# Stick-breaking attention: the causal mask moves from a matrix product into the scan

## The chip, the cores and the metric

The kernel runs on one core of a Trainium2 chip. The metric is the device time of one execution in microseconds, and the median of several runs is given. The engines are TensorE (PE; its weight loads are PEld), VectorE (DVE), ScalarE (ACT), GpSimd (POOL) and SyncE (SP, which here only starts transfers). Each works through its own instructions in a fixed order.

## The reference

Two decoder layers over 512 tokens of width 1024, all in float32. Each layer is a half-step FFN, a mixer, and another half-step FFN, each behind an RMSNorm. Layer 0 mixes with gated linear attention, layer 1 with stick-breaking attention, 16 heads of width 64. Only the second mixer is touched by the change:

```python
z = jnp.einsum('bhtd,bhsd->bhts', q_blk, k).astype(jnp.float32) * scale
mask = s_pos[None, :] < t_pos[:, None]
sp = jnp.where(mask, jax.nn.softplus(z), 0.0)
rem = lax.cumsum(sp, axis=3, reverse=True) - sp
weights = jnp.where(mask, jnp.exp(jax.nn.log_sigmoid(z) - rem), 0.0)
return jnp.einsum('bhts,bhsd->bhtd', weights.astype(v.dtype), v)
```

As `log_sigmoid(z)` is `z - softplus(z)`, a visible weight is `exp(z - S)`, where `S` is the sum of softplus from this key to the last visible one. The mask is strict: a query sees only keys in front of it.

## The kernel before, in words

Every large product is made of three products in a rounded format (a high part times a high part, and the two mixed ones), so each weight tile is split before use: ACT rounds the raw tile to `wh` (line 152) and DVE subtracts to get `wl` (line 153). The products themselves are line 80 (and lines 412 and 779 in the FFNs). Such a split is needed for each 128x1024 piece of weights.

The mixer (class `SB`) runs 17 steps. Step `s` makes the logarithms of the weights of head `s` (`weights_log`) and turns those of head `s-1` into weights (`weights`). After every second head, `values` multiplies two heads by their value vectors. Between these pieces PE is fed with the input and output projections of the mixer by `feed.halves`, so that PE has work while ACT and DVE are busy on a head. `evac_q` and `evac_k` bring the projections of a pair of heads out of PSUM (`n`), and `parts` splits them into `mq`, `kh` and `kl` on ACT and DVE.

The 512 queries of a head are four tiles of 128, and tile `i` needs keys of `i+1` blocks of 128. They are packed into three PSUM tiles `ps_z` of 384, 384 and 512 columns: tile 2; tiles 1 and 0; tile 3. For each of the three, in this order:

- PE makes the logits `z` (line 1486), and adds -1e30 to the masked keys with one more product of an identity `idb` and a triangle `negm` in bfloat16 (`mask`). From step 5 on, the mask of the first two tiles is written first, one step ahead (`masks`).
- ACT makes `|z|` (line 1529), `exp(-|z|)` and `ln(1 + ...)` (through `act`, line 656) into `l`, and `max(z, 0)` into `r` (Relu, line 1532). Their sum is softplus.
- DVE sums from the last key to the first with a scan for each query tile (line 1535), which takes `r` and `l` and adds both at each key, and subtracts the result from the logits (line 1543), which frees the PSUM tile.

One step later PE transposes the result (line 1557), ACT takes the exponential into `wt` (line 656), and `values` uses it (line 1572). ACT then rounds its result to `oh` (line 1581) and DVE makes `ol` (line 1582).

PSUM has three buffers for `ps_z`. The order of the instructions on each engine is fixed when the program is built, by a scheduler that takes code order, priorities and estimated durations; `tc.issue_after` puts an instruction no earlier than another.

Of the kernel before, what the change touches and what calls it, by code (L numbers as in the profile page):

```python
# [10 lines left out]
F32 = mybir.dt.float32  # L11
F32R = mybir.dt.float32r
BF16 = mybir.dt.bfloat16
U8 = mybir.dt.uint8
AF = mybir.ActivationFunctionType
ALU = mybir.AluOpType
PSUM = bass.MemoryType.PSUM

P = 128
T = 512  # L20
# [6 lines left out]
NEG = -1.0e30  # L27
# [3 lines left out]
def turns(t):  # L31

    return t.rearrange("p (two n) -> p n two", two=2)
# [13 lines left out]
def decoder(ctx: ExitStack, tc: tile.TileContext, a: dict, out: bass.AP):  # L47
    nc = tc.nc
# [12 lines left out]
    def psum(name, tag=None):  # L61
        if tag is None:
            tag = order[turn_[0] % 8]
            turn_[0] += 1
        return pp.tile([P, T], F32, tag=tag, bufs=banks[tag], name=name)


    ident = cp.tile([P, P], F32, name="ident")
# [458 lines left out]
    st = {}  # L527
# [125 lines left out]
    def act(o, i, fn, **kw):  # L653

        with tc.issue_after(st["tab"]):
            st["last"] = nc.scalar.activation(o, i, fn, **kw).ins


    class FFN:
# [328 lines left out]
        def run(self, between=None):  # L988
            with tc.tile_pool(name="hp", bufs=8, reuse_waits="tile") as self.hp, tc.tile_pool(
                name="tp", bufs=5, reuse_waits="tile"  # L990
            ) as self.tp:
                st["few"] = self.hp
                new_norm()
                if st["ss"] is not None:
                    if self.after_ffn:
                        exp_ln_tables(st["closed"])
                    two_halves(lambda after: sums_wide(self.tp, after))
                    rstd_wide()
                flush(self.defer)
                def spread(todo, n):  # L1000
                    for i in range(n):
                        for piece in todo[i * len(todo) // n : (i + 1) * len(todo) // n]:
                            with behind(self.last_up):
                                piece()
                        feed.entries(1)

                spread(self.normed_input(), self.NORMED - 2)
                self.normed = True
                st["h"], st["l"] = zip(*self.n)
                st["made"] = [k for j in range(4) for k in (j, j + 4)]  # L1010
                todo = self.sums()
                spread(todo[:5], self.sums_by - self.NORMED)
                feed.entries(1, True)
                for piece in todo[5:]:
                    piece()
                feed.entries(self.count - self.sums_by - 1, True)
                if between is not None:
                    with tc.issue_after(st["closed"]):
                        nc.scalar.preload_act_table_set("sqrt_and_others")
                    feed.q[feed.pos].split()  # L1020
                    between(self.tp)
                feed.entries(self.total - self.count)
# [380 lines left out]
    class SB:  # L1403
# [81 lines left out]
        def logits(self, o_, l_, r_, first, last=False):  # L1485
            nc.tensor.matmul(o_, l_, r_, start=first, stop=last, skip_group_check=True)  # L1486

        def mask(self, bk, ps, first):

            w = self.WID[bk]  # L1490
            m0 = P if bk == 2 else w - P
            nb = (w - m0) // P
            self.logits(
                ps[:, m0:w].rearrange("p (n s) -> p n s", n=nb),
                self.idb,
                self.negm.unsqueeze(1).to_broadcast([P, nb, P]),
                first,
                not first,
            )

        def masks(self, s):


            if self.AHEAD <= s < 16:
                for bk in (1, 2):
                    self.zs[bk] = psum("ps_z", "z")
                    self.mask(bk, self.zs[bk], True)

        def weights_log(self, p, e):

            m = self.qk[p, e, "q"]
            kh, kl = self.qk[p, e, "k"]
            self.ys[p, e] = ys = [None] * 3
            for bk, tiles in ((1, (2,)), (2, (1, 0)), (0, (3,))):
                ahead = bk in self.zs
                ps = self.zs.pop(bk) if ahead else psum("ps_z", "z")
                w = self.WID[bk]
                for n_, i in enumerate(tiles):

                    c0, n = self.BK[i][1], max(2, i + 1) * P  # L1520
                    ts_ = slice(i * P, (i + 1) * P)
                    o_, h_, l_ = ps[:, c0 : c0 + n], turns(kh)[:, 0 : n // 2], turns(kl)[:, 0 : n // 2]
                    self.logits(o_, m[:, ts_], h_, n_ == 0 and not ahead)
                    self.logits(o_, m[:, ts_], l_, False, ahead and i == tiles[-1])
                if not ahead:
                    self.mask(bk, ps, False)
                r = self.hp.tile([P, w], F32, tag=f"r{bk}", name="r")
                l = self.hp.tile([P, w], F32, tag=f"l{bk}", bufs=1, name="l")
                nc.scalar.activation(l, ps[:, 0:w], AF.Abs)
                act(l, l, AF.Exp, scale=-1.0)  # L1530
                act(l, l, AF.Ln, bias=1.0)
                st["relu"] = nc.scalar.activation(r, ps[:, 0:w], AF.Relu).ins
                for i in tiles:
                    c = slice(self.BK[i][1], self.BK[i][1] + (i + 1) * P)
                    nc.vector.tensor_tensor_scan(
                        out=l[:, c][:, ::-1],
                        data0=r[:, c][:, ::-1],
                        data1=l[:, c][:, ::-1],
                        initial=0.0,
                        op0=ALU.add,  # L1540
                        op1=ALU.add,
                    )
                nc.vector.tensor_tensor(out=r, in0=ps[:, 0:w], in1=l, op=ALU.subtract)
                ys[bk] = r
                yield
# [39 lines left out]
        def run(self):  # L1585
            with ExitStack() as es:
                vp = es.enter_context(tc.tile_pool(name="vp2", bufs=1, reuse_waits="tile"))
                self.op = es.enter_context(tc.tile_pool(name="op", bufs=8, reuse_waits="tile"))
                self.qp = es.enter_context(tc.tile_pool(name="qp2", bufs=4, reuse_waits="tile"))
                self.hp = es.enter_context(tc.tile_pool(name="hp3", bufs=2, reuse_waits="tile"))  # L1590
                self.v = [vp.tile([P, D], F32, name=f"w{i}") for i in range(NT)]
                self.ys, self.wt, self.zs = {}, {}, {}
                self.later, self.hold = [], False
                self.idb = vp.tile([P, P], BF16, name="idb")
                self.negm = vp.tile([P, P], BF16, name="negm")
                nc.vector.tensor_copy(self.idb, ident)
                nc.gpsimd.dma_start(self.negm, a["c_neg"])
                new_norm()
                two_halves()
                stats_a("t")  # L1600
                feed.step(2)
                stats_b("t")
                exp_ln_tables(st["sqrt"])
                flush(self.defer)
                feed.step(4)

                steps = [6] * 5 + [5] * 10 + [4] * 2
                self.hold = True
                for s in range(17):
                    p, e = divmod(s, 2)  # L1610
                    q, f = divmod(s - 1, 2)
                    n = steps[s]
                    if s < 16:
                        for i, _ in enumerate(self.weights_log(p, e)):
                            if i != 1:
                                self.parts(st["relu"])
                            if i == 1:
                                k = 2 if n > 4 else 1
                                feed.halves(k)
                                n -= k  # L1620
                    if s > 0:
                        for i, _ in enumerate(self.weights(q, f)):
                            if i < 2:
                                k = min(n, n % 2 if i == 0 and n % 2 else 2)
                                feed.halves(k)
                                n -= k
                            if i == 1:
                                self.masks(s + 1)
                        feed.halves(n)
                        if f == 1:  # L1630
                            self.values(q)
                    else:
                        feed.halves(n)
                feed.entries(self.end + 2 - feed.pos)
# [364 lines left out]
```

## Time and profile before

| | |
|---|---|
| median of 3 runs | 1762.55 us (1762.22 to 1762.95) |
| the profiled execution | 1762.8 us, its span 1760.9 us |
| granted TensorE clock | 0.999 |
| busy share of the span | PE 99%, PEld 93%, DVE 86%, ACT 60%, POOL 3% |
| the 17 steps of the mixer | about 1223 to 1400 us of the span |

A row of instructions names the line, the engine, the operation, what it writes and reads, the shape, how often it ran, the busy time and the mean of one. A row of the timeline begins with start and duration in us; in brackets at its end stand the idle time of the engine before it and what ended that. Records of neighbouring instructions can overlap by a little. In the order of a program, a scan is listed as SCALAR_TENSOR_TENSOR, as the other instructions with three inputs are.

### The profile page before, as it was taken

What the parts mean: (1) busy time and instruction counts of PE and PEld (TensorE: products, weight loads), DVE (VectorE), ACT (ScalarE), POOL (GpSimd) and SP (SyncE); (2) the same over time, 40 slices, a digit from 0 to 9 for tenths busy, and PEclk for the clock granted to TensorE, in tenths of its full rate; (3) what the DMA queues carried; (4) which work ended last, traced back from release to release, by engine and by line L of the source; (5) the groups of instructions that cost most, each with busy time, mean ns of one, the idle gap of its engine ahead of it and who ended that gap; (6) DMA issues with size and microseconds to landing.
All of it is one profiled execution on the core that took longest, in us unless ns stands there. A gap on an engine that the chain in (4) does not pass through costs nothing.

```text
span 1760.9 us, 31387 instructions
## 1 busy us (share of the span) xinstructions
PE 1749.1 (99%) x12714; PEld 1631.3 (93%) x12714; DVE 1509.2 (86%) x2490; ACT 1063.8 (60%) x1899; POOL 55.6 (3%) x77
## 2 busy tenths in 40 slices
PE   9999999999999999999999999999999999999998
PEld 8999999889888999999989999999888889999997
DVE  8999797786888999889798988977898679998886
ACT  7556556554665565555655555655888755565555
POOL 0000000200000000000000000010000000000000
PEclk9999999999999999999999999999999999999999
DMA  5533435422123443444434344352212234434351
GB/s 169 155 113 116 134 107 148 116 65 70 60 79 113 122 118 121 120 121 126 128 98 134 103 126 129 106 133 84 84 49 73 72 96 132 126 102 124 117 146 52
DMA packets 186389, 193.14 MB, mean 110 GB/s; under 512 B 4931, under 2 KB 171125, under 8 KB 186245
## 3 DMA queue, kind: packets, MB, share of 16 engines
q1 hardware_dynamic: 177760, 175.91, 32.0%
q0 software_dynamic: 8240, 14.95, 4.7%
q8 instruction: 99, 1.62, 0.4%
q14 instruction: 46, 0.37, 0.1%
q10 hardware_dynamic: 244, 0.29, 0.0%
HBM read 175.17 MB, written 2.10 MB: 101 GB/s over the span
## 4 chain that ended last, share of the span: by engine, by line
PE 89%; DVE 7%; ACT 3%; DMA 1%; issue 1%; DVEq 0%; SPq 0%
PE ps_w L779 21%; PE ps_d L80 15%; PE ps_f L80 14%; PE ps_q L779 10%; PE ps_z L779 5%; PE ps_w L412 5%; PE ps_b L80 4%; PE ps_t L80 4%; PE ps_q L412 2%; PE ps_z L412 1%; DVE wl L153 1%; PE ps_z L1486 1%; PE ps_oT L1572 1%; PE ps_bt L80 1%; PE ps_T L1557 1%; DMA raw<-in_ffn_w_gate_dram 1%
## 5 line engine op out<-in xcount | busy, mean ns | idle before, releaser
L153 DVE TENSOR_TENSOR wl<-raw,wh 128x1024 fp32r<-128x1024 f32 x241 | 256.4, 1065 | 37.0 <-ACT wh L152 36.2
L152 ACT CAST wh<-raw 128x1024 fp32r<-128x1024 f32 x241 | 222.2, 923 | 70.0 <-PE ps_f L80 23.6
L153 DVE TENSOR_TENSOR wl<-s,wh 128x1024 fp32r<-128x1024 f32 x160 | 195.8, 1224 | 66.2 <-ACT wh L152 65.3
L779 PE MATMUL ps_w<-th,wh 128*128 128x256 f32 x864 | 239.1, 277 | 0.2 <-ACT ps_z L807 0.2
L779 PE MATMUL ps_w<-tl,wh 128*128 128x256 f32 x864 | 237.8, 275 | 0.0
L779 PE MATMUL ps_w<-th,wl 128*128 128x256 f32 x864 | 237.8, 275 | 0.0
L152 ACT CAST wh<-s 128x1024 fp32r<-128x1024 f32 x160 | 168.8, 1055 | 6.0 <-DVE s L765 6.0
L779 PEld LDWEIGHTS ps_w<-th,wh 128*128 128x128 f32 x864 | 165.9, 192 | 1.1 <-ACT ps_z L807 0.4
L80 PE MATMUL ps_f<-xh,wh 128*128 128x512 f32 x432 | 166.5, 386 | 0.0
L779 PEld LDWEIGHTS ps_w<-tl,wh 128*128 128x128 f32 x864 | 166.0, 192 | 0.0
L779 PEld LDWEIGHTS ps_w<-th,wl 128*128 128x128 f32 x864 | 166.0, 192 | 0.0
L80 PE MATMUL ps_f<-xh,wl 128*128 128x512 f32 x432 | 164.3, 380 | 0.5 <-DVE wl L153 0.5
L80 PE MATMUL ps_f<-xl,wh 128*128 128x512 f32 x432 | 164.0, 380 | 0.0
L80 PE MATMUL ps_d<-hh,wh 128*128 128x512 f32 x416 | 157.9, 380 | 0.0
L80 PE MATMUL ps_d<-hh,wl 128*128 128x512 f32 x416 | 157.8, 379 | 0.0
L80 PE MATMUL ps_d<-hl,wh 128*128 128x512 f32 x416 | 157.8, 379 | 0.0
L153 DVE TENSOR_TENSOR wl<-rawd,wh 128x1024 fp32r<-128x1024 f32 (+1 forms) x100 | 96.6, 966 | 9.7 <-ACT wh L152 9.7
L807 ACT COPY ps_z<-ps_w 128x256 f32<-128x256 f32 x72 | 26.0, 362 | 118.3 <-PE ps_w L779 118.1
L363 POOL DMA_DIRECT2D x<-d x53 | 46.0, 911 | 1552.1 <-ACT d L362 1093.5
L80 PEld LDWEIGHTS ps_f<-xl,wh 128*128 128x128 f32 x432 | 81.8, 189 | 11.4
L80 PEld LDWEIGHTS ps_f<-xh,wl 128*128 128x128 f32 x432 | 81.8, 189 | 11.3 <-DVE wl L153 0.9
L80 PEld LDWEIGHTS ps_f<-xh,wh 128*128 128x128 f32 x432 | 81.8, 189 | 10.7
(357 smaller groups left out, 5437.9 us busy)
## 6 DMA issues: line engine op xcount, KB each, us to landing
raw<-in_ffn_w_gate_dram SPq DMA_DIRECT2D x43, 1024.0 KB, 5.5
raw<-in_ffn_w_up_dram SPq DMA_DIRECT2D x43, 1024.0 KB, 5.4
rawd<-in_ffn_w_down_dram SPq DMA_DIRECT2D x84, 512.0 KB, 4.0
x<-d POOLq DMA_DIRECT2D x53, 256.0 KB, 4.6
raw<-in_gla_w_in_dram SPq DMA_DIRECT2D x12, 1024.0 KB, 5.3
raw<-in_sb_w_in_dram SPq DMA_DIRECT2D x16, 512.0 KB, 3.7
raw<-in_gla_w_out_dram SPq DMA_DIRECT2D x4, 1024.0 KB, 5.4
raw<-in_sb_w_in_dram SPq DMA_DIRECT2D x4, 1024.0 KB, 5.1
```

The lines of the kernel that those rows point to most:

```text
L80: st["pe"] = nc.tensor.matmul(ps, l, r, start=first, stop=last).ins
L152: nc.scalar.copy(h[:, k], part)
L153: nc.vector.tensor_tensor(out=l[:, k], in0=part, in1=h[:, k].bitcast(F32), op=ALU.subtract)
L363: nc.gpsimd.dma_start(xs[k], d, accum_op=ALU.add)
L412: st["pe"] = nc.tensor.matmul(ps, l_, r_, start=first and c + n == 0, stop=c == 1 and n == 2, skip_group_check=True).ins
L779: st["pe"] = nc.tensor.matmul(o, l_, r_, start=first and j + n == 0, stop=j == 3 and n == 2, skip_group_check=True).ins
L807: v["copied"] = nc.scalar.copy(z, w).ins
L1486: nc.tensor.matmul(o_, l_, r_, start=first, stop=last, skip_group_check=True)
L1557: nc.tensor.transpose(ps[:, c0 : c0 + P], ys[yb][:, yc + j * P : yc + (j + 1) * P], ident)
L1572: nc.tensor.matmul(po[e * 64 : e * 64 + 64, j * P : T], self.v[j][:, c : c + 64], self.wt[p, e][bk][:, c0 : c0 + n], start=j == 0, stop=j ...
```

## The change

The mask is no longer added to the logits. The scan does the masking: instead of adding `r` and `l` at each key, it multiplies its running value by `keep` and adds `l`. The running value starts at 1e30, `keep` is 1 everywhere except for a 0 at the last visible key of each query. So from the end of the row to that key the running value stays at 1e30, at that key it becomes `l` alone, and from there on it sums. One tile `keep` serves all query tiles, which read different slices of it. As the scan has only two inputs and one of them is now `keep`, softplus must be complete before it: ACT's Relu goes, and a new DVE instruction computes `max(z, 0) + l` from PSUM. The two constants `idb` and `negm` give way to `keep`, made by a GpSimd memset and one DVE instruction ahead of the steps. The casts of `parts` now follow the logarithm (`st["logs"]`) instead of Relu.

```diff
-        def mask(self, bk, ps, first):
-
-            w = self.WID[bk]
-            m0 = P if bk == 2 else w - P
-            nb = (w - m0) // P
-            self.logits(
-                ps[:, m0:w].rearrange("p (n s) -> p n s", n=nb),
-                self.idb,
-                self.negm.unsqueeze(1).to_broadcast([P, nb, P]),
-                first,
-                not first,
-            )
-
-        def masks(self, s):
-
-
-            if self.AHEAD <= s < 16:
-                for bk in (1, 2):
-                    self.zs[bk] = psum("ps_z", "z")
-                    self.mask(bk, self.zs[bk], True)
-
         def weights_log(self, p, e):
...
-                ahead = bk in self.zs
-                ps = self.zs.pop(bk) if ahead else psum("ps_z", "z")
+                ps = psum("ps_z", "z")
...
-                    self.logits(o_, m[:, ts_], h_, n_ == 0 and not ahead)
-                    self.logits(o_, m[:, ts_], l_, False, ahead and i == tiles[-1])
-                if not ahead:
-                    self.mask(bk, ps, False)
+                    self.logits(o_, m[:, ts_], h_, n_ == 0)
+                    self.logits(o_, m[:, ts_], l_, False, i == tiles[-1])
...
                 nc.scalar.activation(l, ps[:, 0:w], AF.Abs)
                 act(l, l, AF.Exp, scale=-1.0)
                 act(l, l, AF.Ln, bias=1.0)
-                st["relu"] = nc.scalar.activation(r, ps[:, 0:w], AF.Relu).ins
+                st["logs"] = st["last"]
+                nc.vector.scalar_tensor_tensor(out=l, in0=ps[:, 0:w], scalar=0.0, in1=l, op0=ALU.max, op1=ALU.add)
                 for i in tiles:
                     c = slice(self.BK[i][1], self.BK[i][1] + (i + 1) * P)
                     nc.vector.tensor_tensor_scan(
                         out=l[:, c][:, ::-1],
-                        data0=r[:, c][:, ::-1],
+                        data0=self.keep[:, T - (i + 1) * P :][:, ::-1],
                         data1=l[:, c][:, ::-1],
-                        initial=0.0,
-                        op0=ALU.add,
+                        initial=-NEG,
+                        op0=ALU.mult,
                         op1=ALU.add,
                     )
...
-                self.idb = vp.tile([P, P], BF16, name="idb")
-                self.negm = vp.tile([P, P], BF16, name="negm")
-                nc.vector.tensor_copy(self.idb, ident)
-                nc.gpsimd.dma_start(self.negm, a["c_neg"])
+                self.keep = vp.tile([P, T], F32, name="keep")
+                nc.gpsimd.memset(self.keep, 1.0)
+                c = slice(T - P - 1, T - 1)
+                nc.vector.tensor_scalar(
+                    out=self.keep[:, c], in0=ident, scalar1=-1.0, scalar2=1.0, op0=ALU.mult, op1=ALU.add
+                )
...
-                                self.parts(st["relu"])
+                                self.parts(st["logs"])
...
-                            if i == 1:
-                                self.masks(s + 1)
```

In the order of the instructions, PE keeps every other instruction in its place. At the start of the steps, the difference on PE (`ps_z<-kh,mq` and `ps_z<-kl,mq` are the logits, `ps_z<-negm,idb` the mask with its own weight load):

```order
 L1486 MATMUL ps_z<-kh,mq 128x384
 L1486 MATMUL ps_z<-kl,mq 128x384
-L1486 LDWEIGHTS idb
-L1486 MATMUL ps_z<-negm,idb 128x128
 L1486 MATMUL ps_z<-kh,mq 128x256
 L1486 MATMUL ps_z<-kl,mq 128x256
 L1486 MATMUL ps_z<-kh,mq 128x256
 L1486 MATMUL ps_z<-kl,mq 128x256
-L1486 LDWEIGHTS idb
-L1486 MATMUL ps_z<-negm,idb 128x256
 L80 MATMUL ps_f<-xh,wh 128x512
```

The logits stand where they stood, and the two masks behind them are gone; the whole program has 48 such pairs fewer.

On DVE in step 1, before the change (`l<-r,l` are the scans, `r<-ps_z,l` the subtractions, `kl`, `n` and `mq` belong to the next pair of heads, `wl` to a weight tile):

```order
L1535 SCALAR_TENSOR_TENSOR l<-r,l 128x384
L1468 CAST kl<-kl 64x512
L1543 TENSOR_TENSOR r<-ps_z,l 128x384
L1467 TENSOR_TENSOR kl<-n,kh 64x512
L1434 SCALAR_TENSOR_TENSOR n<-ps_f,R 128x512
L1468 CAST kl<-kl 64x512
L1535 SCALAR_TENSOR_TENSOR l<-r,l 128x256
L1535 SCALAR_TENSOR_TENSOR l<-r,l 128x128
L153 TENSOR_TENSOR wl<-raw,wh 128x1024
L1543 TENSOR_TENSOR r<-ps_z,l 128x384
```

Each scan or pair of scans follows work of the next heads, and its subtraction comes soon after it. The same place in the changed program, where `l<-ps_z,l` is the new instruction and `l<-keep,l` the scan:

```order
L1509 SCALAR_TENSOR_TENSOR l<-ps_z,l 128x384
L1467 TENSOR_TENSOR kl<-n,kh 64x512
L1512 SCALAR_TENSOR_TENSOR l<-keep,l 128x384
L1468 CAST kl<-kl 64x512
L1520 TENSOR_TENSOR r<-ps_z,l 128x384
L1467 TENSOR_TENSOR kl<-n,kh 64x512
L1509 SCALAR_TENSOR_TENSOR l<-ps_z,l 128x384
L1468 CAST kl<-kl 64x512
L1512 SCALAR_TENSOR_TENSOR l<-keep,l 128x256
L1512 SCALAR_TENSOR_TENSOR l<-keep,l 128x128
L1434 SCALAR_TENSOR_TENSOR n<-ps_f,R 128x512
L1520 TENSOR_TENSOR r<-ps_z,l 128x384
```

Each PSUM tile has gained one instruction in front of its scans, often with another instruction between the two, and the `wl` of this place has moved further back. There are 48 new instructions in all.

More of the change, by code (lines that the diff above doesn't have):

```diff
@@ L1591, in run @@
                 self.v = [vp.tile([P, D], F32, name=f"w{i}") for i in range(NT)]
-                self.ys, self.wt, self.zs = {}, {}, {}
+                self.ys, self.wt = {}, {}
                 self.later, self.hold = [], False
-                self.idb = vp.tile([P, P], BF16, name="idb")
-                self.negm = vp.tile([P, P], BF16, name="negm")
-                nc.vector.tensor_copy(self.idb, ident)
-                nc.gpsimd.dma_start(self.negm, a["c_neg"])
+                self.keep = vp.tile([P, T], F32, name="keep")
[4 more added lines that the diff above has]
+                )
                 new_norm()
```

## The prediction

> **What bounds the kernel now.** I read the page first: shares of the engines, slices, chain.
>
> ```profile
> PE 1749.1 (99%) x12714; PEld 1631.3 (93%) x12714; DVE 1509.2 (86%) x2490; ACT 1063.8 (60%) x1899; POOL 55.6 (3%) x77
> DVE  8999797786888999889798988977898679998886
> PE 89%; DVE 7%; ACT 3%; DMA 1%; issue 1%; DVEq 0%; SPq 0%
> ```
>
> PE is never without work, and the chain that ended last is 89% PE. Read from this alone, whatever PE sheds is gained. But the change works in one stage of a tenth of the span, slices 29 to 32, and there DVE stands at 8, 9, 8 and 6 tenths. So the second view is the table by stretches, over the steps from the first logits (1223.40) to the last subtraction on DVE (1393.64). After the whole stretch I quote two of its parts, one for the pair of steps 6 and 7 and one for the last two steps:
>
> ```profile
> core 0: us, PE busy (x) PEld busy (x) DVE busy (x) ACT busy (x) POOL busy (x), PEclk, DMA share, GB/s
> 1223.40:1393.64 170.24, 169.28 (x1090) 141.80 (x1088) 145.46 (x209) 149.58 (x304) 0.00 (x0) 1.00 0.24 72
> ...
> 1291.07:1312.24 21.17, 20.81 (x129) 17.12 (x128) 20.64 (x32) 19.99 (x41) 0.00 (x0) 1.00 0.17 51
> ...
> 1374.45:1393.64 19.19, 18.71 (x111) 14.55 (x109) 12.77 (x18) 15.17 (x34) 0.00 (x0) 1.00 0.18 55
> ```
>
> PE is busy for 169.3 of 170.2 us: it sets the pace, but DVE has only 24.8 us free, and in steps 6 and 7 half a microsecond. The third view says what the free time is, as DVE's waits in that stretch:
>
> ```profile
> DVE l L1535 <- ACT l L656: 10.5, 12, 1.4
> DVE ol L1582 <- ACT oh L1581: 5.6, 4, 2.2
> DVE n L1434 <- PE ps_f L80: 1.5, 2, 1.3
> DVE mq L1443 <- ACT mq L1480: 1.5, 2, 0.7
> DVE kl L1467 <- ACT kh L1480: 1.3, 3, 0.6
> DVE wl L153 <- ACT wh L152: 0.5, 1, 0.5
> ```
>
> That is 20.9 us of waits for a releaser. The other 3.9 us are short gaps between 209 instructions, no room for anything. DVE's real reserve over these steps is 20.9 us.
>
> The fourth view, the timeline, says how late DVE may be before PE notices. At the end of step 0 and of step 15:
>
> ```profile
> 1235.18 0.69 DVE L1543 TENSOR_TENSOR r<-ps_z,l 128x512 f32<-128x512 f32 x1
> 1236.75 0.23 PE L1486 MATMUL ps_z<-negm,idb 128*128 128x128 bf16 x1
> 1236.82 0.61 PE L1557 MATMUL ps_T<-ident,r 128*128 128x128 f32 x4
> 1392.95 0.69 DVE L1543 TENSOR_TENSOR r<-ps_z,l 128x512 f32<-128x512 f32 x1
> 1393.14 0.88 PE L1557 MATMUL ps_T<-ident,r 128*128 128x128 f32 x6
> ```
>
> The transposes of a head need all its subtractions. At 1236.82 the last one had ended 0.95 us before. Of the six transposes at 1393.14, two belong to step 15 and four to step 16, and these need the subtraction that ends at 1393.64: no margin at all. PE runs in order and has nothing else ready, so a later last subtraction moves the rest of the program by as much.
>
> **PE: 48 masks fewer, about 4.2 us of PE work.** What a mask costs PE is read from the starts, not from the pipelined duration. The one at 1236.75 is followed after 0.07 us by the transposes. For the other two there are two situations:
>
> ```profile
> 1223.68 0.23 PE L1486 MATMUL ps_z<-negm,idb 128*128 128x128 bf16 x1
> 1223.72 0.36 PE L1486 MATMUL ps_z<-kh,mq 128*128 128x256 f32 x1
> 1223.91 0.28 PE L1486 MATMUL ps_z<-kl,mq 128*128 128x256 f32 x1
> 1224.02 0.28 PE L1486 MATMUL ps_z<-kh,mq 128*128 128x256 f32 x1
> 1310.28 0.34 PE L1486 MATMUL ps_z<-negm,idb 128*128 128x128 bf16 x2
> 1310.45 0.38 PE L1557 MATMUL ps_T<-ident,r 128*128 128x128 f32 x2
> ```
>
> In the first five steps a mask and the product behind it take 0.23 us (1223.68 to 1223.91) where such a product alone takes 0.11 (1223.91 to 1224.02): 0.12 us. From step 5 on, the two masks written ahead take 0.17 us together. So 16 x 0.07 + 10 x 0.12 + 11 x 0.17 = 4.2 us, up to 48 x 0.12 = 5.8 if each costs as in the first steps. This shortens the end only while PE is what DVE is waiting for.
>
> **ACT: 48 Relu fewer.**
>
> ```profile
> L1532 ACT ACTIVATE r<-ps_z 128x384 f32<-128x384 f32 x32 | 15.7, 489 | 0.0
> L1532 ACT ACTIVATE r<-ps_z 128x512 f32<-128x512 f32 x16 | 9.7, 608 | 0.0
> ```
>
> ACT loses 25.4 us of records out of 149.6. Of DVE's 20.9 us of waits, 19.4 end with an ACT instruction, so these will shrink. That makes DVE's reserve usable; it does not enlarge it.
>
> **DVE: 48 instructions more.** None of this form (PSUM with a constant, then a second tensor) at 384 columns stands in the trace; its nearest rows are the subtraction, which reads the same two tiles, and `evac_q`, which has the very operation at 512 columns:
>
> ```profile
> L1543 DVE TENSOR_TENSOR r<-ps_z,l 128x384 f32<-128x384 f32 x32 | 17.8, 557 | 1.8
> L1543 DVE TENSOR_TENSOR r<-ps_z,l 128x512 f32<-128x512 f32 x16 | 11.1, 692 | 1.0
> L1434 DVE SCALAR_TENSOR_TENSOR n<-ps_f,R 128x512 f32<-128x512 f32 x7 | 4.8, 690 | 1.6 <-PE ps_f L80 1.5
> ```
>
> 32 x 0.557 + 16 x 0.690 = 28.9 us, which I take. The bounds come from how neighbours follow each other:
>
> ```profile
> 1388.91 0.56 DVE L1543 TENSOR_TENSOR r<-ps_z,l 128x384 f32<-128x384 f32 x1
> 1389.38 0.99 DVE L1535 TENSOR_TENSOR_SCAN l<-r,l 128x256 f32<-128x256 f32 x2
> 1391.62 1.23 DVE L1535 TENSOR_TENSOR_SCAN l<-r,l 128x512 f32<-128x512 f32 x1 [0.58 <-ACT l L656]
> ```
>
> A scan that does not need the subtraction in front of it starts 0.09 us before that one's record ends: 28.9 - 48 x 0.09 = 24.6 us at the least. The subtraction at 1392.95 that needs the scan at 1391.62 starts 0.10 us after that one's record: 28.9 + 48 x 0.10 = 33.7 at the most. [...]
>
> The scans themselves I price at no change: same count, same columns, two SBUF inputs before and after, only the first operation is a multiplication instead of an addition.
>
> ```profile
> L1535 DVE TENSOR_TENSOR_SCAN l<-r,l 128x512 f32<-128x512 f32 x16 | 19.5, 1220 | 4.5 <-ACT l L656 4.5
> L1535 DVE TENSOR_TENSOR_SCAN l<-r,l 128x128 f32<-128x128 f32 x16 | 6.4, 400 | 0.0
> ```
>
> They run at (1220 - 400) / 384 = 2.1 ns a column, twice the (692 - 557) / 128 = 1.05 of the subtraction. A multiplication that ran otherwise is a rival below. [...]
>
> **What costs nothing.** `keep` takes the place of `negm` on POOL's queue at about 1176 us and of `idb` on DVE at about 1198, so the memset has 22 us until DVE needs it; behind it on POOL stands only a transfer of the next FFN. The casts of `parts` follow an ACT instruction that now ends earlier. Without `masks`, PE wants a `ps_z` buffer later than before. Cover gone, each of these is under a microsecond.
>
> **The sum.** DVE must do 28.9 us more in a stretch with 20.9 us of waits. Some waits cannot be filled, since no late work lies in front of them. In step 0 there is no backlog yet:
>
> ```profile
> 1224.98 1.40 DVE L1443 TENSOR_TENSOR mq<-n,mq 64x512 fp32r<-64x512 f32 x2 [0.74 <-ACT mq L1480]
> 1226.96 0.96 DVE L1535 TENSOR_TENSOR_SCAN l<-r,l 128x384 f32<-128x384 f32 x1 [0.57 <-ACT l L656]
> 1229.07 1.22 DVE L153 TENSOR_TENSOR wl<-raw,wh 128x1024 fp32r<-128x1024 f32 x1 [0.49 <-ACT wh L152]
> ...
> 1385.92 0.69 DVE L1582 TENSOR_TENSOR ol<-ps_oT,oh 128x512 fp32r<-128x512 f32 x1 [2.19 <-ACT oh L1581]
> ```
>
> That is 0.74 + 0.57 + 0.49 = 1.8 us. At 1385.92 DVE waits 2.19 us for a result that PE makes in the same step; I leave half of it, 1.1 us, as it is. So the last subtraction comes 28.9 - 20.9 + 1.8 + 1.1 = 10.9 us later, and with no margin there PE too. The 4.2 us saved on PE do not count: PE spends them, and more, waiting for DVE, at the transposes above all. Behind the steps PE is busy without a break, so nothing is won back. The profiled execution took 1762.8 us and would take 1773.7; it lay 0.25 above the median of 1762.55, so I forecast 1773.5 us. The ends: cheapest instructions and every wait filled, 24.6 - 20.9 = +3.7 or 1766; dearest instructions, +15.7 or 1778.
>
> **Rivals.** *The new work hides, and PE keeps the gain.* ACT's relief lets DVE start each scan earlier, what is left of DVE's backlog is never waited for, and the time is 1762.55 - 4.2 = 1758.3. For it: PE at 99%, and the 19.4 us of DVE's waits that end with ACT. Against it: 28.9 does not fit into 20.9, and it would need DVE instructions of under 0.44 us. [...] The same end would come if the scan with a multiplication ran at 1.05 ns a column. Together 5 in 100.
>
> *It balances out*: cheapest instructions, every wait filled and a part of the lateness absorbed, within 0.2%. 4 in 100.
>
> *DVE's queue blocks itself.* The new instruction waits for the logarithm, where before only the scan did, and stands ahead of work of others (`kl`, `wl`, the other tile's scan). If half of the 20.9 us of waits stays or comes back elsewhere, the sum is 28.9 - 10.5 = +18.4, or 1781. For it: 10.5 us of waits for ACT's logarithm now. Against: in the stretch 1291 to 1312 DVE, when late, has no waits left to speak of. It decides if ACT is late too, which loses work. 11 in 100.
>
> **How the numbers follow.** The forecast's mechanism has 80 in 100, nearly all of it between 1766 and 1778. To hold 8 in 10 with the blocked queue's lower half the range is 1766 to 1782. About 0.2% (3.5 us) is what a measurement of this kernel can tell from no change. Faster by more 0.05, within it 0.04, slower 0.91.
>
> **What would show it.** In the profile after: 48 rows of the new instruction at about 0.56 and 0.69 us; scans at 0.40 to 1.22 us as now; DVE's busy time in the steps up by 25 to 30 us with its waits for ACT nearly gone; PE's waits for DVE, 1 us now, at some 15 us in the transposes and the weight splits; last subtraction near 1404. The prediction is wrong if PE still has no such waits, if scans change their duration, or if time moves outside the steps.

## The result, and the profile after

The changed kernel takes 1774.19 us (median of 6 runs, 1773.36 to 1775.57) against 1762.75 for the kernel before (6 runs, 1762.12 to 1764.67): a ratio of 1.0067, with a 95% interval of 1.0057 to 1.0077. The forecast was 1773.5, in a range of 1766 to 1782.

The page of the profiled execution (1774.5 us, span 1772.6) looks almost as before:

```profile
PE 1749.9 (99%) x12666; PEld 1634.6 (92%) x12666; DVE 1531.4 (86%) x2538; ACT 1046.9 (59%) x1851; POOL 55.6 (3%) x77
DVE  8999797787888999898798988977998779998886
PE 86%; DVE 11%; ACT 1%; issue 1%; DMA 1%; DVEq 0%; ACTq 0%
```

PE has 48 instructions fewer and is still busy for 99% of the span. Only the chain tells: DVE's part went from 7% to 11%. The stage shows it. This is the table by stretches over the steps, from the first logits to the last subtraction, as before:

```profile
1223.56:1406.36 182.80, 170.49 (x1042) 144.55 (x1040) 167.47 (x257) 132.87 (x257) 0.00 (x0) 0.97 0.22 67
```

The stretch is 12.6 us longer (182.80 against 170.24) and PE's busy time about the same, so PE now has 12.3 us without work where it had 1.0. DVE is busy for 167.5 instead of 145.5 us, ACT for 16.7 us less. The granted TensorE clock is 0.97 on average; it was 1.00. Outside the stretch little changed: its start is 0.2 us later, and what follows it takes 1.0 us less, for which I have no cause. The waits of the two engines in the stretch, with total, number and the longest:

```profile
DVE l L1509 <- ACT l L656: 4.8, 4, 1.4
DVE ol L1559 <- ACT oh L1558: 3.9, 2, 2.4
DVE wl L153 <- ACT wh L152: 3.2, 3, 2.7
DVE n L1434 <- PE ps_f L80: 1.3, 1, 1.3
```

```profile
PE ps_z L1486 <- DVE r L1520: 11.7, 10, 2.9
PE ps_b L80 <- DVE r L1520: 0.6, 1, 0.6
```

DVE's waits fell from 20.9 to 13.2 us. PE waits in eleven places. In ten of them, 11.7 of the 12.3 us, the first logits into a PSUM buffer wait for the subtraction (line 1520) that frees it; in the last one an output projection (`ps_b`) does. The longest of these waits can be followed on the two timelines, first PE:

```profile
1315.01 0.43 PE L1486 MATMUL ps_z<-kh,mq 128*128 128x384 f32 x1 [1.14 <-DVE r L1520]
1318.55 0.58 PE L1486 MATMUL ps_z<-kh,mq 128*128 128x256 f32 x1 [2.95 <-DVE r L1520]
```

And DVE in the same stretch:

```profile
1314.87 0.55 DVE L1509 SCALAR_TENSOR_TENSOR l<-ps_z,l 128x384 f32<-128x384 f32 x1
1315.33 0.68 DVE L1509 SCALAR_TENSOR_TENSOR l<-ps_z,l 128x512 f32<-128x512 f32 x1
1315.93 0.68 DVE L1512 TENSOR_TENSOR_SCAN l<-keep,l 128x256 f32<-128x256 f32 x1
1316.53 0.40 DVE L1512 TENSOR_TENSOR_SCAN l<-keep,l 128x128 f32<-128x128 f32 x1
1316.84 1.20 DVE L1512 TENSOR_TENSOR_SCAN l<-keep,l 128x512 f32<-128x512 f32 x1
1317.96 0.54 DVE L1520 TENSOR_TENSOR r<-ps_z,l 128x384 f32<-128x384 f32 x1
```

PE needs the subtraction at 1317.96. Its own scans had ended at 1316.93, but the order puts the new instruction and the scan of the next tile (128x512) in front of it, 1.9 us of records, on an engine without a gap. What then happens to PE stands in the clock column (third from the right) of this table:

```profile
1310.00:1316.00 6.00, 4.46 (x29) 3.67 (x27) 5.87 (x10) 5.28 (x10) 0.00 (x0) 1.00 0.30 89
1316.00:1324.00 8.00, 5.45 (x28) 5.45 (x29) 7.91 (x14) 3.72 (x8) 0.00 (x0) 0.57 0.22 65
1324.00:1330.00 6.00, 6.00 (x53) 5.66 (x53) 5.84 (x11) 3.61 (x8) 0.00 (x0) 1.00 0.00 0
```

The clock is at half from 1316.6, still within the longer wait, until 1323.4, and it is so a second time from 1364.4 to 1367.8, behind this wait:

```profile
1363.79 0.38 PE L1486 MATMUL ps_z<-kh,mq 128*128 128x256 f32 x1 [2.23 <-DVE r L1520]
```

The new instruction and the scans (the groups in the stretch; the last row is the scan of 384 columns in the kernel before):

```profile
L1512 DVE TENSOR_TENSOR_SCAN l<-keep,l 128x512 f32<-128x512 f32 x16 | 19.5, 1218 | 0.2
L1509 DVE SCALAR_TENSOR_TENSOR l<-ps_z,l 128x384 f32<-128x384 f32 x32 | 17.4, 554 | 5.2 <-ACT l L656 4.8
L1512 DVE TENSOR_TENSOR_SCAN l<-keep,l 128x384 f32<-128x384 f32 x16 | 15.2, 951 | 0.2
L1509 DVE SCALAR_TENSOR_TENSOR l<-ps_z,l 128x512 f32<-128x512 f32 x16 | 10.8, 676 | 0.0
L1535 DVE TENSOR_TENSOR_SCAN l<-r,l 128x384 f32<-128x384 f32 x16 | 15.2, 951 | 5.4 <-ACT l L656 5.3
```

The scans take what they took: 1218 and 951 ns at 512 and 384 columns, against 1220 and 951. The last subtraction of the steps comes 12.7 us later than before:

```profile
1405.67 0.69 DVE L1520 TENSOR_TENSOR r<-ps_z,l 128x512 f32<-128x512 f32 x1
```

### The profile page after: what moved, and what is told of

The parts are those of the page before. It is cut to its first block, busy times and chain, and to the rows that moved or that the text cites. A ratio compares the mean times of both kernels' runs of the same rounds, so it can differ in the third digit from the quotient of the medians.

```text
span 1772.6 us, 31284 instructions
## 1 busy us (share of the span) xinstructions
PE 1749.9 (99%) x12666; PEld 1634.6 (92%) x12666; DVE 1531.4 (86%) x2538; ACT 1046.9 (59%) x1851; POOL 55.6 (3%) x77
## 4 chain that ended last, share of the span: by engine, by line
PE 86%; DVE 11%; ACT 1%; issue 1%; DMA 1%; DVEq 0%; ACTq 0%
PE ps_w L779 22%; PE ps_d L80 15%; PE ps_f L80 12%; PE ps_q L779 11%; PE ps_z L779 5%; PE ps_w L412 5%; PE ps_b L80 4%; PE ps_t L80 3%; PE ps_q L412 2%; DVE l L1512 2%; DVE wl L153 2%; PE ps_z L412 1%; DVE l L1509 1%; PE ps_bt L80 1%; DVE r L1520 1%
## 5 line engine op out<-in xcount | busy, mean ns | idle before, releaser
L80 PEld LDWEIGHTS ps_f<-xh,wl 128*128 128x128 f32 x432 | 82.2, 190 | 11.5 <-DVE wl L153 0.9
L80 PEld LDWEIGHTS ps_f<-xh,wh 128*128 128x128 f32 x432 | 82.2, 190 | 10.9
```

The source lines that it names most:

```text
L80: st["pe"] = nc.tensor.matmul(ps, l, r, start=first, stop=last).ins
```

## The experiments

The theory was: DVE's added work fills its reserve and the rest comes out at the end. Each kernel ran beside the kernel before on the same chip; that one's median was 1762.2 to 1762.6 us. One thing holds for all of them: a program with another instruction is ordered anew by the scheduler, so a kernel below can differ from the changed one in DVE's order too. Where this matters the text says so.

**One part alone, and each half taken away.** `relu_dve` is the kernel before with

```diff
-                st["relu"] = nc.scalar.activation(r, ps[:, 0:w], AF.Relu).ins
+                st["relu"] = st["last"]
+                nc.vector.tensor_scalar(out=r, in0=ps[:, 0:w], scalar1=0.0, scalar2=None, op0=ALU.max)
```

> The kernel before, with one part of the change alone: max(z, 0) is made on DVE instead of ACT (48 instructions from PSUM), while the masks stay on PE and the scan adds r and l as before. Theory (the mixer's steps become DVE-bound): as slow as the change, 1773 to 1777 us, DVE's waits in the steps down from 20.9 to about 13 us. Rival (the loss comes from the scan with multiplication or from the masks' move): 1762 to 1764 us.

It took 1769.06 us, +6.5: neither expectation. The Relu on DVE alone costs a little over half of what the change costs. The instructions are nearly of the same size (32 of 548 and 16 of 670 ns, 27.3 us, against 28.2), but this Relu needs only the logits, so DVE can do it while ACT is still at the logarithm. DVE's waits in the steps:

```profile
DVE ol L1583 <- ACT oh L1582: 5.3, 3, 2.5
DVE n L1434 <- PE ps_f L80: 1.3, 1, 1.3
DVE l L1536 <- ACT l L656: 1.0, 2, 0.5
DVE r L1533 <- ACT l L1529: 0.5, 2, 0.3
```

Only 1.0 us for the logarithm is left, where the changed kernel has 4.8. All of DVE's waits together are 8.1 us, where about 13 were expected.

`no_new` is the changed kernel without the line

```diff
-                nc.vector.scalar_tensor_tensor(out=l, in0=ps[:, 0:w], scalar=0.0, in1=l, op0=ALU.max, op1=ALU.add)
```

> The changed kernel without its new DVE instruction, so that max(z, 0) is left out of the sum; masks in the scan, no Relu on ACT. Theory: DVE has its old load and PE 4.2 us less, so 1758 to 1760 us, PE without waits for the subtraction. Rival (the scan with multiplication, the new order or the later hold of the PSUM buffers costs the time): 1768 us or more.

1758.48 us, as the theory had it. The multiplying scan and the mask in it cost nothing that shows, since the kernel before without its masks (`no_masks`, next) takes 1758.63; the whole loss hangs on this instruction, 15.7 us.

`no_masks` is the kernel before with `self.mask(...)` never called.

> The kernel before without the 48 mask products (masked keys are left in the sums); DVE and ACT as before. It prices what PE's relief is worth while PE sets the pace: by the starts of the instructions 4.2 us, so 1758.3 us. Rival (DVE and ACT, with the few waits left in the middle steps, are already level with PE): 1761 to 1762.5 us.

1758.63 us, so the masks were worth 3.9 us to PE while it sets the pace; worked out from the starts they were 4.2.

`masks_kept` is the changed kernel with `mask` and `masks` of the kernel before put back, with their constants.

> The changed kernel with the 48 mask products on PE kept besides (the mask is applied twice). Theory: PE waits for DVE in these steps, so 4.2 us more of PE work disappears in its waits: 1773.5 to 1776 us, PE's waits for the subtraction down from about 12 to about 8 us. Rival (PE still sets the time and merely lost something else): 1778.4 us.

1775.53 us, 0.7 above the changed kernel in the last set below and 1.3 above its first median: of 3.9 us of PE work some 3 do not show at the end, within the theory's range. But its reason holds only in part. PE's waits for the subtraction fell from 11.7 to 10.4 us, by 1.3 where 4 were expected:

```profile
PE ps_z L1486 <- DVE r L1544: 10.4, 10, 2.3
```

The clock was at half for 3.4 us here and for 10.2 in the profiled execution of the changed kernel, which gives back another 2.4 us of PE's work.

**Load or place.** After `relu_dve` the question was whether the instruction's work or its place costs. `early` keeps the work and takes it off the way:

```diff
-                nc.vector.scalar_tensor_tensor(out=l, in0=ps[:, 0:w], scalar=0.0, in1=l, op0=ALU.max, op1=ALU.add)
+                nc.vector.scalar_tensor_tensor(out=r, in0=ps[:, 0:w], scalar=0.0, in1=self.keep[:, 0:w], op0=ALU.max, op1=ALU.add)
```

> The changed kernel with the new instruction in place and of the same size, but reading the constant tile instead of the logarithm and writing a tile that nobody reads, so that it waits for the logits alone and the scan does not need it (max(z, 0) is left out of the sum). Theory (DVE's load alone): as slow as the changed kernel, 1773 to 1775 us. Rival (about 5 us of the loss come from where the instruction stands, behind the logarithm and in front of the scan, as Relu on DVE at 1769 suggests): 1766 to 1769 us.

1767.16 us: the theory of load alone fell. With `no_new` at 1758.5, the load is 8.7 us, and the place, with the order that the scheduler makes around it, another 7.0 of the 15.7. That order differs: of the 211 other DVE instructions of the steps, 177 stand in the same order in `early` as in the changed kernel. PE's waits in the steps:

```profile
PE ps_z L1486 <- DVE r L1520: 7.8, 7, 2.2
PE ps_b L80 <- DVE r L1520: 0.6, 1, 0.6
```

So an instruction that no scan needs makes PE wait at the same place, for 8.4 us where the changed kernel has 12.3. The half clock costs 1.7 us of PE's work here and 4.1 there.

`zbuf` gives the loop more room:

```diff
-                ps = psum("ps_z", "z")
+                ps = psum("ps_z", "o" if bk == 0 and e == 1 else "z")
```

> The changed kernel with one more PSUM buffer for the logits: the third tile of every second head goes to the bank of the value products, free at that time. In the changed kernel PE waits 11.7 us at the logits for a buffer that a subtraction has to free. Theory (DVE's work sets the time): the wait only moves to the transposes, which need the same subtractions, 1773 to 1775.5 us. Rival (three buffers make a loop of logits, logarithm, new instruction, scan and subtraction that is too long): 2 to 6 us less than the changed kernel, 1768 to 1772 us.

1770.67 us, 3.5 less, within the rival's range. PE's waits in the steps:

```profile
PE ps_z L1486 <- DVE ol L1559: 4.2, 3, 2.9
PE ps_z L1486 <- DVE r L1520: 3.1, 2, 1.7
PE ps_T L1534 <- DVE r L1520: 1.9, 3, 0.8
```

Some of the waiting did move to the transposes, and some now hangs on `ol`, which frees the borrowed bank; but the sum, with two small waits of the output projections, fell from 12.3 to 9.7 us. In the steps DVE has the same instructions in the same order as in the changed kernel, so no new order there explains the gain: that there are only three buffers for the logits is part of the loss. `add_pool` makes the sum on GpSimd, with Relu back on ACT:

```diff
-                nc.vector.scalar_tensor_tensor(out=l, in0=ps[:, 0:w], scalar=0.0, in1=l, op0=ALU.max, op1=ALU.add)
+                nc.gpsimd.tensor_tensor(out=l, in0=r, in1=l, op=ALU.add)
```

> The changed kernel with Relu back on ACT and the sum of r and l made on GpSimd, which is idle in these steps; DVE gets no new work. Theory: DVE at its old load, PE 4 us less work, so 1759 to 1763 us if GpSimd takes about 1 us an instruction, with some waits from the longer chain. Rival (the longer way through a third engine delays the scans as much as the new DVE instruction did): 1770 us or more.

1774.93 us: the rival. DVE has none of the new instructions and the time is that of the changed kernel. The groups of GpSimd and of two of the scans, and PE's two largest waits, say why:

```profile
L1509 POOL TENSOR_TENSOR l<-r,l 128x384 f32<-128x384 f32 x32 | 40.5, 1267 | 145.4 <-ACT l L656 113.6 <-DVE wl L153 26.1 <-issue 3.7
L1512 DVE TENSOR_TENSOR_SCAN l<-keep,l 128x384 f32<-128x384 f32 x16 | 18.3, 1143 | 9.4 <-POOL l L1509 9.1
L1512 DVE TENSOR_TENSOR_SCAN l<-keep,l 128x128 f32<-128x128 f32 x16 | 8.5, 530 | 0.0
PE ps_T L1534 <- ACT wt L656: 7.4, 6, 3.2
PE ps_z L1486 <- DVE r L1520: 3.9, 5, 2.0
```

Each sum puts 1.3 us (1.4 at 512 columns) on the way from logarithm to scan, and DVE waits 16.8 us for them. Some of DVE's instructions took longer than in the changed kernel, among them the scans of 128 columns, 530 ns on average instead of 405, and the weight splits (`wl`), 1314 instead of 1217. So DVE is not relieved: it is busy for 160.8 us of these steps, against 143.6 in `no_new`. And most of PE's waiting is now for the exponentials of ACT (`wt`), which has its Relu back. The run says that this way through a third engine costs as much as the new DVE instruction; it does not say what the place costs by itself.

**How much each is by itself.** `long_chain` keeps DVE's load at the old level and makes only the way longer, by an ACT copy in place of the instruction:

```diff
-                st["logs"] = st["last"]
-                nc.vector.scalar_tensor_tensor(out=l, in0=ps[:, 0:w], scalar=0.0, in1=l, op0=ALU.max, op1=ALU.add)
+                act(l, l, AF.Copy)
+                st["logs"] = st["last"]
```

> The changed kernel with the new DVE instruction replaced by an ACT copy of the logarithm onto itself (max(z, 0) is left out): the way from logits to subtraction is as long as in the changed kernel, ACT has about the load of before and DVE its old one. Theory (a longer way costs only where DVE has no time to catch up): 1758.5 to 1761 us, like the kernel without the new instruction. Rival (the way's length by itself costs the 7 us between the early and the real instruction): 1764 us or more.

1761.96 us, between the two. `no_masks` has the same number of instructions on PE, ACT and DVE and took 1758.63, and `no_new`, which is this kernel without the copy, 1758.48. From the end of the last logits into a tile to the end of its subtraction, an average of 7.33 us passes here, 6.36 in `no_masks` and 6.64 in `no_new`: 0.7 to 1.0 us more on each tile's way costs 3.3 to 3.5 us even where DVE has its old reserve. The new order is in this difference too. It is about half of the 7.0. In PE's time the profiled executions of `early` and the changed kernel differ by 4.0 us without work and 2.4 us of half clock; what the changed order has in this was not separated.

`early_twice` runs the unread instruction of `early` twice.

> The kernel with the early, unread DVE instruction, which then took 1767.2 us, with that instruction twice: 27 us more of DVE records, on nobody's way (max(z, 0) is left out). Theory (DVE is full by then): most of it comes out at the end, 1786 to 1794 us. Rival (an instruction that nobody waits for is hidden for the most part): under 1778 us.

1784.70 us, 1.3 below the range of the theory and far from the rival. The first 27 us of DVE work cost 8.7 (1758.5 to 1767.2), the next 27 cost 17.5. DVE's waits in the steps show what was left to fill:

```profile
DVE wl L153 <- ACT wh L152: 1.4, 1, 1.4
DVE n L1434 <- PE ps_f L80: 1.3, 1, 1.3
DVE r L1509 <- ACT l L1505: 0.2, 1, 0.2
```

`copies_act` takes other work from DVE:

```diff
-                    nc.vector.tensor_copy(m[oth], t[own])
+                    cast(m[oth], t[own])
...
-                    nc.vector.tensor_copy(l[oth], l[own].bitcast(F32))
+                    cast(l[oth], l[own].bitcast(F32))
```

> The changed kernel with the two copies of each key half (28 of kh and kl each across the steps, 0.42 us apiece, about 12 us) moved from DVE to ACT, which lost Relu. The new instruction stays where it is, behind the logarithm. If the time goes by DVE's load: about 8 to 11 us less than the changed kernel, 1763 to 1766 us. If it goes by the way from the logits to the subtraction: at most 4 us less, 1770 to 1774 us.

1767.79 us, between both. The changed kernel, again beside these,

> The changed kernel again, beside these on the same chip: 1773 to 1776 us.

took 1774.88. So 11.8 us of DVE work less brought 7.1; PE still waits 6.5 us for the subtraction and DVE 13.9 us for the logarithm.

One number puts these kernels in a row. It is the way that `long_chain` was measured by, from the end of the last logits into a tile to the end of its subtraction, as the mean of the 48 tiles in each trace. All of these kernels have three buffers and no mask products on PE:

| kernel | mean way, us | median time, us |
|---|---|---|
| `plain` (below) | 5.75 | 1756.36 |
| `no_masks` | 6.36 | 1758.63 |
| `no_new` | 6.64 | 1758.48 |
| `long_chain` | 7.33 | 1761.96 |
| `early` | 7.75 | 1767.16 |
| `copies_act` | 8.01 | 1767.79 |
| the changed kernel | 8.28 | 1774.19 |
| `add_pool` | 8.81 | 1774.93 |
| `early_twice` | 9.51 | 1784.70 |

Whether the way grew by a dependent instruction or because DVE had more to do, the time went up with it, but for the second and third row, which take the same. `zbuf`, with one more buffer, has 8.62 and took 1770.67. The way contains the tile's waiting for a busy DVE, so the row does not tell load from place. It fits that both come out through the time for which a buffer is held; that this time alone decides is not shown.

**A version that beats both.** `plain` drops the guard for large logits, `exp(-|z|)` and `max(z, 0)`, and has ACT make `ln(1 + exp(z))` in two instructions:

```diff
-                nc.scalar.activation(l, ps[:, 0:w], AF.Abs)
-                act(l, l, AF.Exp, scale=-1.0)
+                act(l, ps[:, 0:w], AF.Exp)
                 act(l, l, AF.Ln, bias=1.0)
                 st["logs"] = st["last"]
-                nc.vector.scalar_tensor_tensor(out=l, in0=ps[:, 0:w], scalar=0.0, in1=l, op0=ALU.max, op1=ALU.add)
```

> The changed kernel with softplus as ln(1 + exp(z)) without the guard for large z: ACT makes two instructions a tile instead of three (four before), DVE none besides scan and subtraction. Theory (DVE back at its old load, ACT far below its own, PE 4 us less): 1758 to 1760 us, faster than both kernels. Rival (something else in the scan's mask costs time): 1765 us or more.

1756.36 us, 1.6 below the theory's range, ratio 0.9966 to the kernel before (0.9953 to 0.9979). Each tile's way has one ACT instruction less than in `no_new`, DVE has its old load, and ACT is busy for 111.6 us of the steps instead of 149.6. The last subtraction ends at 1387.34, 6.3 us earlier than before, and PE has under a microsecond without work up to 0.7 us behind it:

```profile
1223.40:1388.00 164.60, 163.63 (x1040) 140.89 (x1039) 143.78 (x209) 111.64 (x207) 0.00 (x0) 1.00 0.24 75
```

It serves inputs like these; by the formula, a logit so large that `exp(z)` overflows would break it, where the guarded form holds; no run here shows that.

## Why the prediction was right, and where it was not

The direction, the size and the engine were right: PE shed what was forecast, the scan kept its price, the new instruction cost what its neighbours' rows said, and DVE, at 86% of the span, held up PE at 99%. Point by point:

- PE's relief: 4.2 us forecast, 3.9 and 4.1 measured (`no_masks`, and `no_new` against the kernel before). That it does not count while PE waits: some 3 of 3.9 us do not show in `masks_kept`, though its waits took up only 1.3 of them.
- The price of the 48: 28.9 us forecast, 28.2 measured. One new instruction took 554 ns at 384 columns and 676 at 512, where the rows I used had 557 and 690.
- The scans: unchanged, (1218 - 405) / 384 = 2.1 ns a column with a multiplication and an addition, as with two additions ((1220 - 400) / 384). Why a scan takes twice the subtraction's 1.05 ns a column, no run here shows.
- The last subtraction: forecast 10.9 us later, found 12.7 (1406.36 against 1393.64).

The term that failed is "some waits cannot be filled", which I set at 1.8 + 1.1 us. DVE's waits in the steps are 13.2, and 11.9 of them still end with an ACT instruction, where I had these nearly gone. The longest is one of step 0, where a `wl` now stands in front of `mq` and waits 2.7 us for its `wh`:

```profile
1227.15 1.23 DVE L153 TENSOR_TENSOR wl<-raw,wh 128x1024 fp32r<-128x1024 f32 x1 [2.74 <-ACT wh L152]
```

The total held because the other term was too high: DVE's busy time rose by 22.0, not by 28.9, since records overlap (by 0.08 to 0.09 us between neighbours in the six rows from 1314.87 on), and the short gaps shrank from 3.9 to 2.1. So 22.0 - 1.8 - 7.7 (waits filled) = 12.5, where the forecast had 28.9 - 20.9 + 2.9 = 10.9. Two errors of opposite sign met, so that the sum came this close is luck. The sum also has no term for the clock, which cost 4.1 us of PE's work.

Behind that stands a step of reasoning: that DVE's total decides. `early` has this load and costs 8.7 us, not 15.7. The prediction gave the blocked queue, an instruction that waits for the logarithm ahead of other work, 11 in 100 as a rival, priced to come out at 1781. By `early`, its place and the order around it are 7.0 of the 15.7: DVE waits 13.2 us in the steps of the changed kernel and 7.0 in those of `early`, 4.8 against 0.9 of them for the logarithm. So what that rival names did happen: over half of the 20.9 us of waits stayed. Its 1781 was not reached because DVE's busy time rose by 22.0 and not by 28.9.

And the place of PE's wait was wrong: I named the transposes and the weight splits. It is the logits, for one of three PSUM buffers: the mean way from logits to subtraction, for which a buffer is held, grew from 6.37 to 8.28 us. I had called the removal of `masks` free because PE wants a buffer later than before. The subtractions fell behind by more than that.

From PE's side: 11.3 us more without work (12.3 against 1.0), 4.1 us lost at half clock (PE busy from 1318.55 to 1323.4 and from 1364.4 to 1367.8, half of each), less 3.9 for the masks, is 11.5 of the 12.6 found; for the other 1.1 I have no cause. By the traces PE's order is not wholly the old one either, other than said with the change: near the end of the steps, six products of the output projection and two transposes stand earlier.

## What to carry to other kernels

Work may be moved off the engine that sets the pace only onto a reserve that is there in that stage: read the busy time and the waits of the stretch, not the share of the span. Even then ask where the moved instruction stands: one that can start as soon as its input is there cost 8.7 us here, one of the same size between the logarithm and the scan 15.7, each with the order that the scheduler made around it. And where few buffers close a loop between engines, measure for how long a buffer is held: 0.7 to 1.0 us more on the way cost over 3 us in `long_chain`. The version with the shortest way, which also gives ACT the least work, was the fastest (1756.4 us); moving the sum from engine to engine was not.

## What the runs showed of the hardware that was not expected

Some waits of PE cost more than their length. In the changed kernel, after waits of 1.14 and 2.95 us with little between, the same products followed each other at 0.21 us instead of 0.11, and the granted clock was 0.5 for 4.9 us after PE was back at work; a single wait of 2.23 us ending at 1363.79 was followed by 3.4 us of it. The waits of 1.70 and 0.96 us at the start of the steps were not: the clock stayed at 1.00. Their length does not decide alone: in `masks_kept` a wait of 1.85 us that ended at 1327.90 was followed by half clock from 1329.2 to 1332.6, and in `add_pool` one of 3.17 us that ended at 1295.31 by none. Eight such stretches stand in the steps of six of these traces. Five lasted 3.4 us (one each in the changed kernel, `masks_kept`, `early`, `relu_dve` and `add_pool`) and three 6.8 us (the changed kernel, `zbuf` and `add_pool`). What decides whether a wait is followed by one, no run here shows.

DVE's scans took longer in `add_pool`, where GpSimd works on other tiles at the same time: 530 ns on average at 128 columns, 405 in the changed kernel, and 1143 at 384, where the changed kernel has 951. The run has its own comparison. The 13 scans of 384 columns whose records overlap one of GpSimd took 1186 ns on average, the three others 957; but four of the 13 took 1.65 to 1.75 us and nine 0.96, like those alone. At 128 columns four that overlap took 918 ns on average and the twelve others 400. No scan of 512 columns met GpSimd, and these stayed at 1219. The subtractions of 384 columns, which read PSUM and one tile of SBUF, took 557 ns beside GpSimd and 555 alone. So an overlap did not always go with a longer scan, and what made the few longer, no run here shows.
